# Masked attention on one core: a new order and new queues for the first loads, transposes moved inside the loop, and a merged last group

## The chip, the core and the metric

The kernel runs on one core of a Trainium2 chip. The time is the device time of the run in microseconds (us), as a median over several runs. The profile is of one execution; its span is about 2 us shorter than the run's time, since it counts from the first to the last instruction. The engines are called as in the profile: PE (matrix multiply), PEld (its weight loads, which overlap it: 272.5 and 194.8 us busy in a span of 302.5 before), DVE (vector), ACT (exponential), POOL (which issues the software-queue transfers), SP (which issues the stores).

## The reference

```python
B, S, D = 2, 3328, 128            # mask: (B, S, S) fp32, 64 ones in each row
logits = np.matmul(q, k.transpose(0, 2, 1)) * D ** -0.5
logits = np.where(mask == 0, -1e9, logits)
attn = np.exp(logits - logits.max(axis=-1, keepdims=True))
return np.matmul(attn / attn.sum(axis=-1, keepdims=True), v)
```

The mask is dense in memory: 88.6 of the 98.8 MB that the kernel reads.

## The kernel before

Each batch has 26 tiles of 128 rows. A *group* is 1, 2 or 4 query tiles (128, 256 or 512 wide) and walks over the 26 key tiles, the *chunks*, two at a time. PE adds `32768 * mask` to the logits by multiplying the mask with a scaled identity; the exponential's bias takes the 32768 off again. A column of ones beside v yields the sum for the division. Loads of q, k, v and mask are cast from fp32 to bf16 by the software queue.

```python
plans = [plan_groups([256, 256, 512, 512, 512, 512, 512, 256]),
         plan_groups([512, 512, 512, 512, 512, 512, 128, 128])]
...
def emit_transposes(b, which, half):              # 4 tiles ("a quad") per PSUM slot
    for t4 in range(h0, h1, 4):
        n = min(4, h1 - t4)
        tp = main_psum.tile([P, 4, P], bf16, name="stp", bufs=3)
        for i in range(n):
            nc.tensor.transpose(tp[:, i, :], nat[:, t4 + i, :], identb)
        nc.vector.tensor_copy(dst[:, t4 : t4 + n, :], tp[:, 0:n, :])
...
for c0 in range(0, NT, CPAIR):                    # emit_group_compute, a pair of chunks
    stp = main_psum.tile([P, CPAIR, 512], fp32, name="stp", bufs=3)
    ...   # PE, per chunk: kt x qt, then one mask matmul for each query tile
    ...   # ACT: one exponential if w == 512, else one for each chunk
    ...   # PE: pt x vones for each chunk and query tile
...
qkv_b(0, "k", 0); qkv_b(0, "k", 1); qkv_b(0, "q", 0); qkv_b(0, "q", 1)
...                                               # all transposes of batch 0
emit_mask_piece(0, 0, msks0[0], 0, 2)             # first half (13 chunks) of group 0's masks
qkv_b(0, "v", 0); qkv_b(0, "v", 1)
emit_mask_piece(0, 0, msks0[0], 1, 2)
...
for g in range(ng0): ... emit_group_compute(0, g, msks0[g])
...                                               # all transposes of batch 1
for g in range(ng1): ... emit_group_compute(1, g, msks1[g])
```

The groups' logits and the quads of transposes share three PSUM slots.

The softmax here doesn't subtract the row's maximum and nothing guards it: scores larger than these inputs give would overflow.

## Time and profile before

| | |
|---|---|
| median of 5 runs | 304.53 us (304.28 to 305.94) |
| span of the profiled run | 302.5 us |
| first exponential | 19.41 us |
| end of group 0 | 33.8 us |
| a 512-wide group of four tiles | 20.17 us |
| two 128-wide groups at the end | 13.35 us |

These are lines of the page of the kernel before: busy time of each engine as a share of the span, then the span in 40 slices of 7.56 us in tenths, then the chain of work that ended last.

```profile
PE 272.5 (90%) x3224; PEld 194.8 (64%) x3224; DVE 32.7 (11%) x139; ACT 197.8 (65%) x274; POOL 70.0 (23%) x124
...
PE   0677989999999999999998999999999999999895
...
ACT  1035986766766667666882676666766766667794
...
PEclk9999999999999999999999999999999999999998
DMA  7999999999999999999999999999999995010010
...
PE 56%; ACT 28%; DMA 6%; issue 4%; POOL 3%; DVE 1%; ACTq 0%; DVEq 0%; POOLq 0%
```

PE and the DMA engines both look full. Which one holds the time? PE's stages are read best from the divisions at the end of each group. In these lines of the timeline of DVE in the kernel before (start, duration, engine, line, operation, output and input; in brackets the idle time before it and what ended that) the first division of a group stands for the group's end.

```profile
33.78 0.17 DVE L213 RECIPROCAL recip<-ov 128x1 f32<-128x1 f32 x1 [17.09 <-PE ov L202]
...
45.95 0.17 DVE L213 RECIPROCAL recip<-ov 128x1 f32<-128x1 f32 x1 [11.15 <-PE ov L202]
...
127.19 0.17 DVE L213 RECIPROCAL recip<-ov 128x1 f32<-128x1 f32 x1 [18.43 <-PE ov L202]
...
147.64 0.17 DVE L213 RECIPROCAL recip<-ov 128x1 f32<-128x1 f32 x1 [18.71 <-PE ov L202]
...
184.88 0.17 DVE L213 RECIPROCAL recip<-ov 128x1 f32<-128x1 f32 x1 [21.19 <-PE ov L202]
...
285.71 0.17 DVE L213 RECIPROCAL recip<-ov 128x1 f32<-128x1 f32 x1 [18.43 <-PE ov L202]
...
299.06 0.17 DVE L213 RECIPROCAL recip<-ov 128x1 f32<-128x1 f32 x1 [6.15 <-PE ov L202]
```

Between two 512-wide groups there are 20.17 us, while mask half-tiles follow each other every 2.0 to 2.1 us, which is 16 to 17 us for four tiles. PE, with ACT in its loop, sets the middle, and DMA keeps ahead. The time outside that pace is in three places. (1) The head, until 33.78. (2) The boundary between the batches: groups 6 and 7 of batch 0 and group 0 of batch 1 end at 147.64, 158.77 and 184.88. (3) The tail after 285.71. The head's waits are in the timeline of PEld before:

```profile
7.59 1.30 PEld L124 LDWEIGHTS <-k_nat 128*128 128x128 bf16 x13 [7.59 <-DMA k_nat<-in_k_dram]
...
16.67 0.10 PEld L172 LDWEIGHTS <-msk 128*128 128x128 bf16 x1 [0.63 <-DMA msk<-in_mask_dram]
...
18.66 0.10 PEld L172 LDWEIGHTS <-msk 128*128 128x128 bf16 x1 [1.85 <-DMA msk<-in_mask_dram]
...
27.86 0.11 PEld L172 LDWEIGHTS <-msk 128*128 128x128 bf16 x2 [2.05 <-DMA msk<-in_mask_dram]
```

The first mask halves come behind all of k and q, and the second halves, last of ten transfers, are there only at 27.86. The timeline of ACT shows the other two places: 6.06 us without an exponential at the boundary, and a tail in which 52 exponentials follow each other without a gap, 0.264 us each.

```profile
164.41 2.12 ACT L182 ACTIVATE pt<-stp,bias_tile 128x1024 bf16<-128x1024 f32 x2 [6.06 <-PE stp L172]
...
285.00 13.73 ACT L191 ACTIVATE pt<-stp,bias_tile 128x128 bf16<-128x128 f32 x52
```

### The profile page before, as it was taken

The page shows a single profiled execution, that of the slowest core. Times are in us where ns is not written, and L with a number is a line of the kernel's source. Part 1 is how long each engine was busy: PE and PEld are TensorE (multiplying, and loading weights), DVE is VectorE, ACT ScalarE, POOL GpSimd, SP SyncE. Part 2 cuts the span into 40 slices and gives each one's busy share as a digit, 9 for nine tenths or more (in the row PEclk, how much of TensorE's full clock was granted, in tenths as well). Part 3 has the DMA queues.
Part 4 walks back from the last instruction along what each step waited for, and adds up shares of the span by engine and source line. Part 5 has one row for each costly group of instructions (what it writes and reads, how often), then busy time and mean ns, then how long its engine had stood idle before and what let it go on. Part 6 is the DMA issues. An engine that isn't in the chain of part 4 may idle for free.

```text
span 302.5 us, 7431 instructions
## 1 busy us (share of the span) xinstructions
PE 272.5 (90%) x3224; PEld 194.8 (64%) x3224; DVE 32.7 (11%) x139; ACT 197.8 (65%) x274; POOL 70.0 (23%) x124
## 2 busy tenths in 40 slices
PE   0677989999999999999998999999999999999895
PEld 0555656667676766666766666667667666676662
DVE  0510101010020020100216002002020020020200
ACT  1035986766766667666882676666766766667794
POOL 9522222222222224512222222222222200000000
PEclk9999999999999999999999999999999999999998
DMA  7999999999999999999999999999999995010010
GB/s 73 190 193 214 212 215 214 214 212 216 214 213 217 214 214 217 206 189 189 214 215 214 216 211 212 218 214 213 217 214 214 217 212 124 2 37 0 11 38 9
DMA packets 42656, 53.30 MB, mean 176 GB/s; under 512 B 22656, under 2 KB 29312, under 8 KB 42624
## 3 DMA queue, kind: packets, MB, share of 16 engines
q0 software_dynamic: 35136, 49.42, 91.2%
q1 hardware_dynamic: 7488, 3.41, 5.3%
q8 instruction: 25, 0.41, 0.5%
q14 instruction: 7, 0.06, 0.0%
HBM read 98.83 MB, written 3.41 MB: 338 GB/s over the span
## 4 chain that ended last, share of the span: by engine, by line
PE 56%; ACT 28%; DMA 6%; issue 4%; POOL 3%; DVE 1%; ACTq 0%; DVEq 0%; POOLq 0%
PE ov L202 35%; ACT pt L182 25%; PE stp L172 13%; PE stp L164 8%; DMA msk<-in_mask_dram 6%; ACT pt L191 3%; POOL k_nat L110 1%; POOL vones L99 1%; POOL q_nat L110 1%; DVE qt L125 1%; POOL msk L136 1%; DVE kt L125 0%; ACTq L182 0%; DVE o_sb L215 0%; ACTq L191 0%
## 5 line engine op out<-in xcount | busy, mean ns | idle before, releaser
L182 ACT ACTIVATE pt<-stp,bias_tile 128x1024 bf16<-128x1024 f32 x143 | 152.0, 1110 | 76.2 <-PE stp L172 76.2
L172 PE MATMUL stp<-bigident,msk 128*128 128x128 bf16 x1352 | 160.4, 220 | 3.4 <-DMA msk<-in_mask_dram 3.3
L164 PE MATMUL stp<-qt,kt 128*128 128x512 bf16 (+2 forms) x416 | 139.1, 342 | 0.3 <-ACT pt L191 0.2
L202 PE MATMUL ov<-vones,pt 128*128 128x129 bf16 x1352 | 122.5, 222 | 12.2 <-ACT pt L182 1.6
L202 PEld LDWEIGHTS <-pt 128*128 128x128 bf16 x1352 | 80.0, 98 | 67.3 <-ACT pt L182 49.8
L172 PEld LDWEIGHTS <-msk 128*128 128x128 bf16 x1352 | 106.7, 98 | 24.4 <-DMA msk<-in_mask_dram 4.8
L136 POOL DMA_DIRECT2D msk<-in_mask_dram x104 | 55.2, 532 | 161.6 <-DMA msk<-in_mask_dram 108.8
L191 ACT ACTIVATE pt<-stp,bias_tile 128x256 bf16<-128x256 f32 (+1 forms) x130 | 44.7, 481 | 23.8 <-PE stp L172 21.7
L164 PEld LDWEIGHTS <-kt 128*128 128x128 bf16 x416 | 41.1, 99 | 0.1
L213 DVE RECIPROCAL recip<-ov 128x1 f32<-128x1 f32 x52 | 7.3, 158 | 246.4 <-PE ov L202 246.4
L215 DVE TENSOR_SCALAR o_sb<-ov,recip 128x128 f32<-128x128 f32 x52 | 17.2, 348 | 1.0
L124 PE MATMUL stp<-identb,k_nat 128*128 128x128 bf16 x52 | 5.8, 264 | 8.8 <-DMA k_nat<-in_k_dram 8.4
L124 PEld LDWEIGHTS <-k_nat 128*128 128x128 bf16 x52 | 4.3, 120 | 9.2 <-DMA k_nat<-in_k_dram 8.6
L125 DVE COPY kt<-stp 128x512 bf16<-128x512 bf16 (+1 forms) x16 | 5.5, 370 | 16.7 <-PE stp L124 16.7
L124 PE MATMUL stp<-identb,q_nat 128*128 128x128 bf16 x52 | 5.4, 265 | 1.8 <-DMA q_nat<-in_q_dram 1.5
L124 PEld LDWEIGHTS <-q_nat 128*128 128x128 bf16 x52 | 4.3, 121 | 3.1 <-DMA q_nat<-in_q_dram 2.1
L125 DVE COPY qt<-stp 128x512 bf16<-128x512 bf16 (+1 forms) x16 | 5.2, 369 | 1.9 <-PE stp L124 1.9
L110 POOL DMA_DIRECT2D k_nat<-in_k_dram x4 | 4.7, 1176 | 2.8 <-DMA msk<-in_mask_dram 2.8
L110 POOL DMA_DIRECT2D q_nat<-in_q_dram x4 | 4.6, 1144 | 3.0 <-DMA msk<-in_mask_dram 3.0
L99 POOL DMA_DIRECT2D vones<-in_v_dram x4 | 4.6, 1163 | 1.7 <-DMA msk<-in_mask_dram 1.7
L191 ACT ACT_TABLE_LOAD x1 | 1.3, 1283 | 1.0 <-DVE bias_tile L82 1.0
masks.py:199 POOL TENSOR_SCALAR_AFFINE_SELECT identb<-identb 128x128 bf16<-128x128 bf16 x1 | 0.3, 282 | 0.0
(9 smaller groups left out, 1.3 us busy)
## 6 DMA issues: line engine op xcount, KB each, us to landing
msk<-in_mask_dram POOLq DMA_DIRECT2D x104, 416.0 KB, 16.7
out_dram<-o_sb SPq DMA_DIRECT2D x52, 64.0 KB, 8.1
k_nat<-in_k_dram POOLq DMA_DIRECT2D x4, 416.0 KB, 12.3
q_nat<-in_q_dram POOLq DMA_DIRECT2D x4, 416.0 KB, 13.5
vones<-in_v_dram POOLq DMA_DIRECT2D x4, 416.0 KB, 16.7
```

Source lines behind the costliest of these rows:

```text
L99: nc.gpsimd.dma_start(out=voness[b][:, h0:h1, 0:P], in_=v[b, h0 * P : h1 * P, :].rearrange("(t p) d -> p t d", p=P),)
L110: nc.gpsimd.dma_start(out=nat[:, h0:h1, :], in_=src_t[b, h0 * P : h1 * P, :].rearrange("(t p) d -> p t d", p=P),)
L124: nc.tensor.transpose(tp[:, i, :], nat[:, t4 + i, :], identb)
L125: nc.vector.tensor_copy(dst[:, t4 : t4 + n, :], tp[:, 0:n, :])
L136: nc.gpsimd.dma_start(out=msks[j][:, c0:c1, :], in_=mask[b, q0 + j * P : q0 + (j + 1) * P, c0 * P : c1 * P].rearrange("p (t c) -> p t c", ...
L164: nc.tensor.matmul(stp[:, ci, 0:w], kt[:, c, :], qt[:, t0 : t0 + nsub, :], start=True, stop=False,)
L172: nc.tensor.matmul(stp[:, ci, j * P : (j + 1) * P], msks[j][:, c, :], bigident, start=False, stop=(j == nsub - 1),)
L182: nc.scalar.activation(out=pt[:, 0:ncp, :], in_=stp[:, 0:ncp, :], func=mybir.ActivationFunctionType.Exp, bias=bias_tile, scale=softmax_scale,)
L191: nc.scalar.activation(out=pt[:, ci, 0:w], in_=stp[:, ci, 0:w], func=mybir.ActivationFunctionType.Exp, bias=bias_tile, scale=softmax_scale,)
L202: nc.tensor.matmul(ovs[j // 2][:, j % 2, 0:129], pt[:, ci, j * P : (j + 1) * P], vones[:, c, 0:129], start=(c == 0 and j % 2 == 0), stop=( ...
L213: nc.vector.reciprocal(recip, ov[:, 128:129])
L215: nc.vector.tensor_scalar_mul(o_sb, ov[:, 0:P], recip)
```

## The change

Its intent is to start the first group earlier, to keep the exponentials going at the boundary, and to shorten the tail. (a) **Head:** only 4 of 26 q tiles are loaded before group 0. They and all of k come as fp32 by the hardware queues of ACT and SP and are cast by DVE. v and masks alternate on the software queue. The second part of k is transposed inside group 0, the other q tiles inside groups 1 to 3. (b) **Boundary:** batch 1's 14 quads go between the chunk pairs of groups 6 and 7. (c) **Tail:** one 256-wide group instead of two of 128.

```diff
-            plan_groups([512, 512, 512, 512, 512, 512, 128, 128]),
+            plan_groups([512, 512, 512, 512, 512, 512, 256]),
...
         for c0 in range(0, NT, CPAIR):
+            if (b, g) == (0, 0):
+                if c0 == 8:
+                    cast_hw("k", KH, NT, k1, first_copies)
+                    while quads:
+                        emit_quad(*quads.pop(0))
+            elif quads and c0 >= quads_from:
+                emit_quad(*quads.pop(0))
...
+    KH = 12
-    qkv_b(0, "k", 0)
-    qkv_b(0, "k", 1)
-    qkv_b(0, "q", 0)
-    qkv_b(0, "q", 1)
...
+    k0 = load_hw("k", 0, KH, nc.sync)
+    q0s = load_hw("q", 0, 4, nc.scalar)
+    k1 = load_hw("k", KH, NT, nc.sync)
+    load_v(0, 6)
     emit_mask_piece(0, 0, msks0[0], 0, 2)
-    qkv_b(0, "v", 0)
-    qkv_b(0, "v", 1)
+    load_v(6, 13)
     emit_mask_piece(0, 0, msks0[0], 1, 2)
...
+    load_v(13, 26)
+    emit_mask_piece(0, 1, msks0[1], 0, 2)
+    emit_mask_piece(0, 1, msks0[1], 1, 2)
+    load_q_sw(4, 8)
...
+    load_q_sw(8, 16)
+    cast_hw("q", 0, 4, q0s)
+    cast_hw("k", 0, KH, k0)
+    for quad in quads_of("q", 0, 4) + quads_of("k", 0, KH):
+        first_copies = emit_quad(*quad)
+    early_quads = {
+        0: quads_of("k", KH, NT),
+        1: quads_of("q", 4, 8),
+        2: quads_of("q", 8, 16),
+        3: quads_of("q", 16, 26),
+    }
...
-        emit_group_compute(0, g, msks0[g])
-    emit_transposes(1, "k", 0)
...
+        emit_group_compute(
+            0, g, msks0[g],
+            quads if g >= ng0 - 2 else early_quads.get(g),
+            quads_from={ng0 - 2: 16, ng0 - 1: 4}.get(g, 18),
+        )
```

More of the change, by code (lines that the diff above doesn't have):

```diff
@@ L120, in emit_transposes, with emit_quad @@
         for t4 in range(h0, h1, 4):
-            n = min(4, h1 - t4)
-            tp = main_psum.tile([P, 4, P], bf16, name="stp", bufs=3)
-            for i in range(n):
-                nc.tensor.transpose(tp[:, i, :], nat[:, t4 + i, :], identb)
-            nc.vector.tensor_copy(dst[:, t4 : t4 + n, :], tp[:, 0:n, :])
+            emit_quad(nat, dst, t4, min(4, h1 - t4))
+    def emit_quad(nat, dst, t4, n):
+        tp = main_psum.tile([P, 4, P], bf16, name="stp", bufs=3)
+        for i in range(n):
+            nc.tensor.transpose(tp[:, i, :], nat[:, t4 + i, :], identb)
+        return nc.vector.tensor_copy(dst[:, t4 : t4 + n, :], tp[:, 0:n, :])
     def emit_ones_col(b):
@@ L146, in make_group_msks, with emit_group_compute @@
         return [mask_pool.tile([P, NT, P], bf16, name="msk") for _ in range(nsub)]
-    def emit_group_compute(b, g, msks):
+    def emit_group_compute(b, g, msks, quads=None, quads_from=4):
         kt, qt, vones = kts[b], qts[b], voness[b]
@@ L223, in qkv_b, with nat_of @@
         load_qkv_half(b, which, half)
-    emit_ones_col(0)
-    qkv_b(0, "k", 0)
-    qkv_b(0, "k", 1)
-    qkv_b(0, "q", 0)
-    qkv_b(0, "q", 1)
-    emit_transposes(0, "k", 0)
-    emit_transposes(0, "k", 1)
-    emit_transposes(0, "q", 0)
-    emit_transposes(0, "q", 1)
+    def nat_of(which):
+        if (0, which) not in nat_cache:
+            nm = {"q": "q_nat", "k": "k_nat"}[which]
+            nat_cache[(0, which)] = stage_pool.tile([P, NT, P], bf16, name=nm, bufs=1)
+        return nat_cache[(0, which)]
@@ new lines, in rows_of, with load_hw, cast_hw @@
+    def rows_of(src, b, h0, h1):
+        return src[b, h0 * P : h1 * P, :].rearrange("(t p) d -> p t d", p=P)
+    def load_hw(which, h0, h1, eng):
+        st = stage_pool.tile([P, h1 - h0, P], fp32, name=f"st_{which}{h0}", bufs=1)
+        eng.dma_start(out=st, in_=rows_of({"q": q, "k": k}[which], 0, h0, h1))
+        return st
+    def cast_hw(which, h0, h1, st, behind=None):
+        cast = nc.vector.tensor_copy(nat_of(which)[:, h0:h1, :], st)
+        if behind is not None:
+            tc.add_manual_dep(
+                cast.ins,
+                behind.ins.name,
+                mybir.DependencyInfo(
+                    mybir.DependencyClass.NoSync, mybir.DependencyReason.DATA
+                ),
+                reason="keep the late cast behind the early copies",
+            )
@@ new lines, in load_v, with load_q_sw, quads_of @@
+    def load_v(h0, h1):
+        nc.gpsimd.dma_start(out=voness[0][:, h0:h1, 0:P], in_=rows_of(v, 0, h0, h1))
+    def load_q_sw(h0, h1):
+        nc.gpsimd.dma_start(out=nat_of("q")[:, h0:h1, :], in_=rows_of(q, 0, h0, h1))
+    def quads_of(which, h0, h1):
+        dst = {"q": qts[0], "k": kts[0]}[which]
+        return [(nat_of(which), dst, t4, min(4, h1 - t4)) for t4 in range(h0, h1, 4)]
+    KH = 12
+    emit_ones_col(0)
+    k0 = load_hw("k", 0, KH, nc.sync)
+    q0s = load_hw("q", 0, 4, nc.scalar)
@@ L234 @@
+    k1 = load_hw("k", KH, NT, nc.sync)
+    load_v(0, 6)
     emit_mask_piece(0, 0, msks0[0], 0, 2)
-    qkv_b(0, "v", 0)
-    qkv_b(0, "v", 1)
+    load_v(6, 13)
     emit_mask_piece(0, 0, msks0[0], 1, 2)
-    for pc in range(2):
-        emit_mask_piece(0, 1, msks0[1], pc, 2)
+    load_v(13, 26)
+    emit_mask_piece(0, 1, msks0[1], 0, 2)
+    emit_mask_piece(0, 1, msks0[1], 1, 2)
+    load_q_sw(4, 8)
     for pc in range(2):
         emit_mask_piece(0, 2, msks0[2], pc, 2)
+    load_q_sw(8, 16)
@@ L254 @@
                 qkv_b(1, b1_qkv_parts[2 * idx + 1][0], b1_qkv_parts[2 * idx + 1][1])
-        emit_group_compute(0, g, msks0[g])
-    emit_transposes(1, "k", 0)
-    emit_transposes(1, "k", 1)
-    emit_transposes(1, "q", 0)
-    emit_transposes(1, "q", 1)
+        if g == ng0 - 2:
+            quads = [
+                (nat_cache[(1, which)], dsts[1], t4, min(4, NT - t4))
+                for which, dsts in (("k", kts), ("q", qts))
+                for t4 in range(0, NT, 4)
+            ]
+        if g == 0:
+            load_q_sw(16, 26)
+        emit_group_compute(
+            0,
+            g,
+            msks0[g],
+            quads if g >= ng0 - 2 else early_quads.get(g),
+            quads_from={ng0 - 2: 16, ng0 - 1: 4}.get(g, 18),
+        )
+    for quad in quads:
+        emit_quad(*quad)
     for pc in range(2):
```

## The prediction

> **What bounds it now.** The page gives PE 90% busy, ACT 65%, and the DMA engines at nine tenths or more of nearly every slice until 253 us. Yet in steady state DMA is ahead: a 512-wide group of four mask tiles takes 20.17 us on PE (spacing of the output divisions, e.g. 66.69 to 86.86), while mask half-tiles land every 2.0 to 2.1 us, about 16.6 us a group. So the middle is bound by PE with ACT in its loop (chain of waits: PE 56%, ACT 28%, mask DMA 6%), and the removable time lies at three places in the timeline:
>
> 1. Head. Nothing but transposes runs on PE until 16.2 us; then mask waits last until 27.86, and group 0 ends at 33.8. Ten transfers must land first (four k/q halves and two v halves at 2.34 us each, four mask halves at 2.0).
> 2. Batch boundary. From the end of group 6 of batch 0 (147.64) to the end of group 0 of batch 1 (184.88) is 37.24 us. Its 256-wide group takes about 11.1 and its 512-wide one 20.17; some 6 us are the 14 serial transpose-and-copy quads (ACT idle 6.06 us before 164.41).
> 3. Tail. Two 128-wide groups take 13.35 us, bound by ACT (52 exponentials, 13.73). A 256-wide group takes 11.1 to 12.2.
>
> **What changes.**
> - Head: only q rows of 4 of 26 tiles precede group 0, saving about 3.9 us of transfer, and k comes by hardware queues that start sooner (the first software packet moves at 3.6 us). First masks should land at 9 to 11 us, not 16.7 to 18.7. But the hardware queue shares the engines with masks. [...] The trace agrees: a 128-row output store takes 2.3 us among masks, interleaved with 127 to 131 mask packets, against 0.32 us alone. So the second k part (112 rows per engine, my arithmetic) moves slowly whenever masks flow: my estimate is landing at 18 to 30 us. Group 0 stalls for it at chunk 8 to 12. The DVE casts add an estimated 1 to 2 us. I expect group 0 to end at 28 to 33 (30), a gain of about 4.
> - Early q quads: six move from the DMA-bound head into the PE-bound groups 1 to 3. A quad is 0.22 us on PE (4 x 56 ns) and takes one of three PSUM slots; estimate 0.25 us each, loss 1.5.
> - Boundary: 14 quads move into groups 6 and 7. PE waits for ACT about 0.3 us per chunk pair in the 256-wide group, so quads mostly fit there; in the 512-wide group I estimate 0.3 each. Of 6 us some 4 are gained.
> - Tail: 1.5 us gained.
>
> **Sum:** 304.5 - 4 + 1.5 - 4 - 1.5 = 296.5 us; range 290 to 302. Faster by over 2%: 0.64; within: 0.31; slower: 0.05.
>
> **What would show it.** First exponential before 13 us (was 19.4); first output division near 30 (33.8). A PE wait on the k copies or casts inside group 0. Group 6 to batch 1 group 0 about 33 us, with no 6 us ACT idle; groups 2 and 3 about 0.5 to 0.8 longer than 20.17; last group about 12 us. DMA bytes written up by about 1 MB, ending near 250.
>
> **What would make it wrong.** Masks starving the second k part past 30 us: group 0 then ends no earlier, and the head gains nothing. Quads stalling the PSUM rotation by more than 0.5 us each: the boundary gain goes. In the other direction: hardware rows that keep pace with the masks (group 0 ending at 27) and quads that fit wholly into PE's waits would give 290.

## The result, and the profile after

The changed kernel takes 296.67 us (median of 8 runs, 296.51 to 296.87); the kernel before, in the same rounds, 304.53 (15 runs). The ratio is 0.9729, 95% interval 0.9713 to 0.9746. All ratios here are the mean time of one kernel's fast runs over that of the other's of the same rounds, so not quite the ratio of the medians.

The same lines of the page of the changed kernel:

```profile
PE 266.5 (90%) x3198; PEld 192.0 (65%) x3198; DVE 36.0 (12%) x138; ACT 195.8 (66%) x248; POOL 69.6 (24%) x124
...
PE   0499999999999999999999999999999999999994
...
ACT  1068876667676767666777767676766667676784
...
PEclk9999999999999999999999999999999999999997
DMA  7999999999999999999999999999999999410010
...
PE 52%; ACT 29%; DMA 11%; issue 4%; POOL 2%; ACTq 1%; DVE 0%; POOLq 0%
```

The shares of busy time hardly moved, and the idle slices at the start became fewer. In the chain that ended last DMA has 11% instead of 6%. The list of that chain in order of time (start, duration) shows why. Before, one mask load stands in it, from 10.22 us for 17.59 us. After, there are two, one after the other:

```profile
6.82 17.96 DMA msk<-in_mask_dram
25.07 15.79 DMA msk<-in_mask_dram
```

The second ends in a PE wait at 40.90, for a mask of group 2. So in this profile the chain runs through the arrival of masks up to there, and not through the work of groups 0 and 1. The stages tell more. The divisions in the timeline of DVE after:

```profile
28.96 0.17 DVE L222 RECIPROCAL recip<-ov 128x1 f32<-128x1 f32 x1 [8.29 <-PE ov L211]
...
41.62 0.17 DVE L222 RECIPROCAL recip<-ov 128x1 f32<-128x1 f32 x1 [4.42 <-PE ov L211]
...
123.62 0.17 DVE L222 RECIPROCAL recip<-ov 128x1 f32<-128x1 f32 x1 [18.43 <-PE ov L211]
...
144.74 0.17 DVE L222 RECIPROCAL recip<-ov 128x1 f32<-128x1 f32 x1 [2.73 <-PE ov L211]
...
179.16 0.17 DVE L222 RECIPROCAL recip<-ov 128x1 f32<-128x1 f32 x1 [19.74 <-PE ov L211]
...
280.17 0.17 DVE L222 RECIPROCAL recip<-ov 128x1 f32<-128x1 f32 x1 [18.44 <-PE ov L211]
...
291.27 0.17 DVE L222 RECIPROCAL recip<-ov 128x1 f32<-128x1 f32 x1 [9.38 <-PE ov L211]
```

Differences of such lines give the table, in us from one group's end to the next; "batch 1, group 0" includes what was left of the boundary.

| stage | before | after | change |
|---|---|---|---|
| until the end of group 0 | 33.78 | 28.96 | -4.82 |
| group 1 (256 wide, 1 quad moved in) | 12.17 | 12.66 | +0.49 |
| group 2 (2 quads) | 20.74 | 21.12 | +0.38 |
| group 3 (3 quads) | 20.17 | 20.54 | +0.37 |
| group 6 (5 quads) | 20.45 | 21.12 | +0.67 |
| group 7 (256 wide, 9 quads) | 11.13 | 13.67 | +2.54 |
| batch 1, group 0 | 26.11 | 20.75 | -5.36 |
| tail (two groups, then one), to its last group's division | 13.35 | 11.10 | -2.25 |

The seven other groups moved by at most 0.15 us. Head -4.8, moved q quads +1.2, boundary -2.2, tail -2.2, and +0.3 in the rest and the last stores: that is the 7.7 us between the spans. Not all of the 1.2 us is the quads' price: 0.46 of group 1's 0.49 is the wait at 40.90, the last line below. In `e3_head`, a run below with the same quads and without that wait, the three groups grew by 0.11, 0.37 and 0.36 us, 0.8 together. The head's waits, in the timeline of PEld after:

```profile
7.18 0.34 PEld L126 LDWEIGHTS <-q_nat 128*128 128x128 bf16 x4 [7.18 <-DVE q_nat L249]
8.05 1.20 PEld L126 LDWEIGHTS <-k_nat 128*128 128x128 bf16 x12 [0.52 <-DVE k_nat L249]
...
13.06 0.24 PEld L181 LDWEIGHTS <-msk 128*128 128x128 bf16 x3 [3.35 <-DMA msk<-in_mask_dram]
14.93 0.10 PEld L181 LDWEIGHTS <-msk 128*128 128x128 bf16 x1 [1.64 <-DMA msk<-in_mask_dram]
...
40.90 0.10 PEld L181 LDWEIGHTS <-msk 128*128 128x128 bf16 x1 [0.46 <-DMA msk<-in_mask_dram]
```

PE waits for q and the first k until 8.05, then for the first masks until 13.06 and 14.93. The second k part doesn't appear as a wait at all: DVE began to cast it at 15.49, as soon as it had landed and before group 0 could use it. One more thing slows the head, which the page does not show (its PEclk row reads 9 from the start): PE itself. In the same timeline a weight load takes 0.15 us at first and 0.10 us later:

```profile
16.84 0.15 PEld L173 LDWEIGHTS <-kt 128*128 128x128 bf16 x1
...
20.12 0.10 PEld L173 LDWEIGHTS <-kt 128*128 128x128 bf16 x1
```

The change comes at 18.8 us, and at 23.2 in the kernel before. It comes at 17.9, 18.0 and 20.5 us in three other profiles with the same head (`e6_octets`, `e7_twice`, `e3_head`, all below), where group 0 ended at 28.60, 28.66 and 29.67. Weight loads are slower again in `e1_tail` (below) where the granted clock dips: 30 of them keep PEld busy for 2.75 us there, at a granted 0.68, and 48 for 2.77 in `e2_boundary`, at 1.00. So this looks like PE's clock. Group 0's end thus carries a spread of about 1 us that no edit made. The tail in the timeline of ACT after has one short gap and 26 exponentials:

```profile
279.45 3.02 ACT L200 ACTIVATE pt<-stp,bias_tile 128x256 bf16<-128x256 f32 x8
282.98 7.92 ACT L200 ACTIVATE pt<-stp,bias_tile 128x256 bf16<-128x256 f32 x18 [0.50 <-PE stp L181]
```

### The profile page after: what moved, and what is told of

The parts are those of the page before. It is cut to its first block, busy times and chain, and to the rows that moved or that the text cites. A ratio compares the mean times of both kernels' runs of the same rounds, so it can differ in the third digit from the quotient of the medians.

```text
span 294.8 us, 7345 instructions
## 1 busy us (share of the span) xinstructions
PE 266.5 (90%) x3198; PEld 192.0 (65%) x3198; DVE 36.0 (12%) x138; ACT 195.8 (66%) x248; POOL 69.6 (24%) x124
## 4 chain that ended last, share of the span: by engine, by line
PE 52%; ACT 29%; DMA 11%; issue 4%; POOL 2%; ACTq 1%; DVE 0%; POOLq 0%
PE ov L211 32%; ACT pt L191 26%; PE stp L181 12%; DMA msk<-in_mask_dram 11%; PE stp L173 7%; ACT pt L200 3%; POOL vones L261 1%; POOL msk L138 1%; PE stp L126 1%; ACTq L191 0%; DVE o_sb L224 0%; ACTq L366 0%; DVE recip L222 0%; POOL identb masks.py:199 0%; POOL bigident L71 0%
## 5 line engine op out<-in xcount | busy, mean ns | idle before, releaser
L181 PE MATMUL stp<-bigident,msk 128*128 128x128 bf16 x1352 | 158.0, 220 | 4.3 <-DMA msk<-in_mask_dram 4.3
L173 PE MATMUL stp<-qt,kt 128*128 128x512 bf16 (+1 forms) x390 | 136.6, 353 | 0.1
L211 PE MATMUL ov<-vones,pt 128*128 128x129 bf16 x1352 | 118.1, 222 | 12.7 <-ACT pt L191 1.6
L211 PEld LDWEIGHTS <-pt 128*128 128x128 bf16 x1352 | 78.4, 98 | 64.6 <-ACT pt L191 47.0
L138 POOL DMA_DIRECT2D msk<-in_mask_dram x104 | 56.1, 540 | 158.0 <-DMA msk<-in_mask_dram 110.6
L200 ACT ACTIVATE pt<-stp,bias_tile 128x256 bf16<-128x256 f32 x104 | 42.1, 476 | 21.6 <-PE stp L181 18.7
L173 PEld LDWEIGHTS <-kt 128*128 128x128 bf16 x390 | 38.4, 99 | 0.1
L264 POOL DMA_DIRECT2D q_nat<-in_q_dram x3 | 2.6, 868 | 4.1 <-DMA msk<-in_mask_dram 3.1
L110 POOL DMA_DIRECT2D k_nat<-in_k_dram x2 | 2.3, 1145 | 4.8 <-issue 2.8
L249 DVE CAST k_nat<-st_k 128x1536 bf16<-128x1536 f32 (+1 forms) x2 | 2.0, 1024 | 5.5 <-DMA st_k<-in_k_dram 5.5
```

What stands on the lines that cost most here:

```text
L138: nc.gpsimd.dma_start(out=msks[j][:, c0:c1, :], in_=mask[b, q0 + j * P : q0 + (j + 1) * P, c0 * P : c1 * P].rearrange("p (t c) -> p t c", ...
L173: nc.tensor.matmul(stp[:, ci, 0:w], kt[:, c, :], qt[:, t0 : t0 + nsub, :], start=True, stop=False,)
L181: nc.tensor.matmul(stp[:, ci, j * P : (j + 1) * P], msks[j][:, c, :], bigident, start=False, stop=(j == nsub - 1),)
L200: nc.scalar.activation(out=pt[:, ci, 0:w], in_=stp[:, ci, 0:w], func=mybir.ActivationFunctionType.Exp, bias=bias_tile, scale=softmax_scale,)
L211: nc.tensor.matmul(ovs[j // 2][:, j % 2, 0:129], pt[:, ci, j * P : (j + 1) * P], vones[:, c, 0:129], start=(c == 0 and j % 2 == 0), stop=( ...
L264: nc.gpsimd.dma_start(out=nat_of("q")[:, h0:h1, :], in_=rows_of(q, 0, h0, h1))
```

## The experiments

All twelve gave correct results and ran beside the kernel before on the same chip.

### One part at a time

`e1_tail`, `e2_boundary` and `e3_head` are the kernel before with one of the three parts:

```diff
 e1_tail:     plan_groups([512, 512, 512, 512, 512, 512, 256])     # nothing else
 e2_boundary: before's head and tail; quads of batch 1 in groups 6 and 7
 e3_head:     before's tail and boundary; new loads, casts, q quads in groups 1 to 3
```

> Only the last plan changes: one 256-wide group for two of 128. If the three parts of the change are independent, the time falls by the 2.2 us that the tail gained in the two profiles (285.71 to 302.5 before, 280.17 to 294.8 after): ratio about 0.993. If the tail's gain was only the shorter wait after other parts moved, less than 1 us.

> Only the transposes of batch 1 move into groups 6 and 7 of batch 0. By the profiles the boundary gained 57.69 - 55.54 = 2.15 us from group 6 to the first group of batch 1: ratio about 0.993. The prediction's 4 us would give 0.987.

> Only the head changes (order of loads, hardware queues and casts, late q transposes). By the profiles group 0 ends 4.8 us earlier and groups 1 to 3 lose 1.2 us: net 3.6 us, ratio about 0.988. The three parts should sum to the whole, 7.9 us, within 0.6 us.

| run | median us (range) | ratio to before (95%) |
|---|---|---|
| `e1_tail` | 303.09 (302.43 to 304.21) | 0.994 (0.9901 to 0.998) |
| `e2_boundary` | 303.0 (302.23 to 303.94) | 0.9944 (0.9901 to 0.9987) |
| `e3_head` | 300.26 (300.2 to 300.51) | 0.9845 (0.9815 to 0.9875) |

The savings add: 0.6 + 0.56 + 1.55 = 2.71%, the same as the whole. The stages agree: in `e1_tail` the tail's group takes 11.10 us; in `e2_boundary` the three boundary stages take 21.39 + 13.66 + 20.74; in `e3_head` group 0 ends at 29.67. The 0.987 that the prediction's 4 us at the boundary would give lies outside `e2_boundary`'s interval. The head is more than half of it. The first two intervals are wide, about 1.2 us to each side, so the sum alone does not prove that the parts are independent.

Those wide intervals show something else. With the old head, runs fall on two levels, in the kernel before too: of the 7 runs beside these, four lie at 304.16 to 304.42 and three at 305.5 to 306.0. The profile of `e1_tail` caught an upper run (304.21), that of `e2_boundary` a lower one (302.23). These are windows of 4 us around the end of the last mask wait (the stretch and its length; busy us and number of instructions of PE, PEld, DVE, ACT and POOL; granted clock of PE; DMA share; GB/s), first `e1_tail`:

```profile
24.00:28.00 4.00, 1.88 (x22) 1.03 (x19) 0.00 (x0) 1.23 (x4) 0.79 (x2) 1.00 1.07 212
28.00:32.00 4.00, 3.42 (x29) 2.75 (x30) 0.00 (x0) 3.06 (x8) 1.06 (x2) 0.68 1.08 213
32.00:36.00 4.00, 4.00 (x51) 3.39 (x50) 0.44 (x3) 3.33 (x10) 1.06 (x2) 0.89 1.07 212
```

and then `e2_boundary`:

```profile
24.00:28.00 4.00, 2.76 (x32) 2.08 (x30) 0.00 (x0) 1.68 (x4) 0.63 (x2) 1.00 1.07 211
28.00:32.00 4.00, 3.85 (x50) 2.77 (x48) 0.00 (x0) 3.85 (x11) 1.06 (x2) 1.00 1.07 211
32.00:36.00 4.00, 3.90 (x51) 2.88 (x51) 0.94 (x4) 3.74 (x11) 1.06 (x2) 1.00 1.07 212
```

In the upper run PE was granted 0.68 and 0.89 of its clock in the 8 us after the wait, and group 0 ended at 35.52 instead of 33.74. Of these 1.78 us some 0.6 are the mask's own lateness (the wait ended at 28.45 against 27.82). The record agrees for the other runs: the mean granted clock of every upper run is 0.989 to 0.994, that of every lower one 0.995 to 0.999. The same dip stands in two more profiles, `e9_late_one_exp` (0.89 and 0.68 from 24 to 32 us) and `e11_quarters_two_exp` (0.61 from 24 to 28; its weight loads take 0.15 us from 23.88 to 27.00). The runs of `e3_head` and of the changed kernel lie within 0.4 us of each other; they have no such wait amid group 0. That is worth more than the stages of the profile (a lower-level run) show: part of `e3_head`'s 1.55% is these slow starts. Within a level, `e1_tail` and `e2_boundary` are each 1.8 to 2.0 us below the kernel before (302.43 and 302.23 against 304.3), and `e3_head` is 4.0 below it. Together that is 7.8 us, where the changed kernel is 7.7 below: within a level the parts do add. Why one run falls on the upper level and another on the lower was not tested.

### Hardware queues or order?

`e4_head_sw` keeps the new order, but uses the software queue alone:

```diff
-    k0 = load_hw("k", 0, KH, nc.sync)
-    q0s = load_hw("q", 0, 4, nc.scalar)
-    k1 = load_hw("k", KH, NT, nc.sync)
+    load_sw("q", 0, 4)          # cast by the DMA, into q_nat and k_nat
+    load_sw("k", 0, KH)
+    load_sw("k", KH, NT)
...                              # the three DVE casts go
```

> The changed kernel, but all first k and q loads go in the same order by the software queue, cast by the DMA, with no DVE casts. Theory A (the head gained by the hardware queues starting early, at 1.7 us instead of 3.6): group 0 ends about 2 us later than in the changed kernel, near 31, ratio to before about 0.98. Theory B (it gained by putting fewer bytes before the masks, whichever queue carries them): group 0 ends within 0.7 us of 28.96, ratio about 0.973.

It took 297.93 us (297.75 to 298.09), ratio 0.9767; group 0 ended at 29.84. Of the head's 4.8 us, 3.9 are still there (33.78 - 29.84), and the hardware queues are worth at most about 1 us: 0.9 in group 0's end, 1.3 in the medians (with intervals that overlap). That is nearer theory B, but a little outside its 0.7. Against the four profiles with the hardware queues, where group 0 ended at 28.60 to 29.67 and group 1 at 41.62 to 41.95, it is 0.2 to 1.2 us (29.84) and 0.3 to 0.6 us (42.23), so the exact size is not settled. The order of bytes is most of the gain. In the trace, the hardware queues move their first row at 1.8 us and the software queue here at 3.2; yet PE has the first k part at 8.05 with them and at 8.34 without.

### What stands before the masks

The prediction feared that masks would starve the second k part. The profile after shows the reverse. `e5_k1_late` puts that part behind the first masks:

```diff
-    k1 = load_hw("k", KH, NT, nc.sync)
-    load_v(0, 6)
     emit_mask_piece(0, 0, msks0[0], 0, 2)
+    load_v(0, 6)
+    load_sw("k", KH, NT)
```

> The changed kernel, but the second part of k goes by the software queue, cast by the DMA, behind the first mask halves and the first part of v; the rest of the order stays. Theory A (group 0 starts when its first masks land, and the second k part stands ahead of them, 112 rows per engine or about 2.5 to 3 us): the first exponential comes near 12.5 to 13.5 us instead of 15.7, group 0 ends near 26.5 instead of 28.96, the time is near 294.5. Rival (all bytes that group 0 needs must land anyway, and it ends when the last of them has): the first exponential is earlier, but group 0 waits for k or the later masks inside and ends within 0.6 us of 28.96, time within 0.6 us of 296.7.

It took 295.76 us (295.68 to 295.99), ratio 0.9693. The waits of PEld, in its timeline:

```profile
10.35 0.10 PEld L180 LDWEIGHTS <-msk 128*128 128x128 bf16 x1 [0.29 <-DMA msk<-in_mask_dram]
...
13.99 0.17 PEld L126 LDWEIGHTS <-k_nat 128*128 128x128 bf16 x3 [0.40 <-DMA k_nat<-in_k_dram]
...
19.29 0.10 PEld L180 LDWEIGHTS <-msk 128*128 128x128 bf16 x1 [1.72 <-DMA msk<-in_mask_dram]
...
39.92 0.10 PEld L180 LDWEIGHTS <-msk 128*128 128x128 bf16 x1 [1.14 <-DMA msk<-in_mask_dram]
```

PE's last wait for the first mask halves ends at 10.35 instead of 14.93, and the first exponential comes at 11.11 instead of 15.69, earlier than theory A expected. Theory A's cause is right, but its size is not: group 0 ends at 27.28, a gain of 1.7, not 2.5, because it now waits for k (0.40) and for the second mask half (1.72). Group 1 takes 13.35 instead of 12.66 because a mask of group 2 is late (1.14). Of 4.6 us at the start, 0.9 are left in the time. The rest fits the rival: past the start, PE waited inside the groups for bytes that landed later (the 0.40, 1.72 and 1.14 us above).

### What a quad costs at the boundary

The boundary gained 2.2 us and not 4. Its three stages still cost 4.1 us more than 20.17 + 11.1 + 20.17. Two causes were possible: PE's own time, or the PSUM slot that each quad takes from the rotation. `e6_octets` keeps the 52 transposes but uses 8 slots instead of 14; `e7_twice` keeps the slots and doubles the transposes.

```diff
 e6_octets:
-        tp = main_psum.tile([P, 4, P], bf16, name="stp", bufs=3)
+        tp = main_psum.tile([P, max(n, 4), P], bf16, name="stp", bufs=3)
...
-                (nat_cache[(1, which)], dsts[1], t4, min(4, NT - t4))
+                (nat_cache[(1, which)], dsts[1], t8, min(8, NT - t8))
 e7_twice:
         for i in range(n):
-            nc.tensor.transpose(tp[:, i, :], nat[:, t4 + i, :], identb)
+            for _ in range(2 if dst is kts[1] or dst is qts[1] else 1):
+                nc.tensor.transpose(tp[:, i, :], nat[:, t4 + i, :], identb)
```

> The changed kernel, but the transposes of batch 1 go eight to a PSUM slot with one copy, so 8 slots instead of 14, with the same 52 transposes. Groups 6, 7 and the first of batch 1 take 21.12 + 13.67 + 20.75 = 55.54 us in the changed kernel, some 4.1 more than 20.17 + 11.1 + 20.17. If that cost is PSUM slots taken out of the rotation, it falls with their number, to about 2.3 (sum 53.8, time near 295). If it is PE time (52 x 56 ns = 2.9 us), the sum stays within 0.5 us of 55.5.

> The changed kernel, but each transpose of batch 1 is done twice into the same place: 52 more transposes (2.9 us of PE at 56 ns), same slots and copies. If the boundary's remaining cost is PE time, the sum of the three groups rises by about 2.9 us to 58.4 and the time to 299.5. If PE has waits into which they fit and slots are the cost, it rises by less than 1 us.

| run | group 6 | group 7 | batch 1, group 0 | sum | median us |
|---|---|---|---|---|---|
| changed kernel | 21.12 | 13.67 | 20.75 | 55.54 | 296.67 |
| `e6_octets` | 22.15 | 12.76 | 20.75 | 55.66 | 297.03 (ratio 0.9733) |
| `e7_twice` | 22.83 | 15.14 | 20.75 | 58.72 | 299.91 (ratio 0.9828) |

Fewer slots changed nothing. 52 more transposes cost 3.18 us, 61 ns each, a little more than the 56 ns at which transposes follow each other on PE in the trace. So it is PE's time, and over the three stages it counts in full: about 2.9 of the 4.1 us left. It is not spread evenly: the 20 further transposes in group 6 cost 1.71 us (86 ns each), the 32 in group 7 cost 1.47 (46 ns each), so in group 7 a small part does hide. What makes up the other 1.2 us was not tested. The lines of `e7_twice` behind the sum, with the timeline of DVE as above:

```profile
123.71 0.17 DVE L223 RECIPROCAL recip<-ov 128x1 f32<-128x1 f32 x1 [18.43 <-PE ov L212]
...
146.54 0.17 DVE L223 RECIPROCAL recip<-ov 128x1 f32<-128x1 f32 x1 [3.03 <-PE ov L212]
...
161.68 0.17 DVE L223 RECIPROCAL recip<-ov 128x1 f32<-128x1 f32 x1 [3.73 <-PE ov L212]
...
182.43 0.17 DVE L223 RECIPROCAL recip<-ov 128x1 f32<-128x1 f32 x1 [19.73 <-PE ov L212]
```

### A version that beats both: shorter loops, then finer loads

`e8_one_exp` changes the 256-wide groups, which no part of the change touched: one exponential for a pair of chunks.

```diff
-            if w == 512:
-                ...                 # one exponential
-            else:
-                for ci in range(ncp):
-                    ...             # one for each chunk
+            nc.scalar.activation(out=pt[:, 0:ncp, 0:w], in_=stp[:, 0:ncp, 0:w], ...)
```

> The changed kernel, but the 256-wide groups do one exponential per pair of chunks (128x512 elements) instead of two. From starts of back-to-back exponentials (0.264 us at 128 columns, 0.384 at 256, 1.06 at 1024) I estimate 0.61 us instead of 0.77 a pair. If ACT's time bounds these groups, each of the four shortens by up to 2 us (13 pairs x 0.16): time near 289 to 292, last group near 9.5 instead of 11.10. If the loop PE-ACT-PE bounds them, the later start of the exponential (it waits for both chunks) cancels it: within 1 us of 296.7, or slower.

295.26 us (293.81 to 295.36), ratio 0.9664. Group 7 took 12.23 instead of 13.67 and the last 10.03 instead of 11.10: 1.44 and 1.07 us. An exponential of 128x512 takes 0.68 us, and back to back it starts 0.585 us after the one before it, so the 0.61 that I estimated was close. But in the second half of the last group the exponentials start 0.77 to 0.80 us apart, against 0.97 for a pair of two in the changed kernel: 0.18 a pair, and 1.07 us over the whole group. What holds them at 0.79 was not tested. Group 1 ended no earlier (41.55 against 41.62): PE waited 1.87 us for a mask of group 2 there. Here, too, runs fall on two levels, 293.81 once and 295.2 to 295.36 three times; the head has waits again.

`e9_late_one_exp` joins the last two. `e10_quarters` also brings the masks of groups 0 to 2 in quarters; `e11_quarters_two_exp` is that with the two exponentials of before; `e12_early_qk` moves three loads of q and k ahead of masks.

```diff
 e10_quarters, against e9_late_one_exp:
-    emit_mask_piece(0, 0, msks0[0], 0, 2)
+    emit_mask_piece(0, 0, msks0[0], 0, 4)
     load_v(0, 6)
+    emit_mask_piece(0, 0, msks0[0], 1, 4)
     load_sw("k", KH, NT)
     load_v(6, 13)
-    emit_mask_piece(0, 0, msks0[0], 1, 2)
+    emit_mask_piece(0, 0, msks0[0], 2, 4)
     load_v(13, 26)
+    emit_mask_piece(0, 0, msks0[0], 3, 4)
...                                     # groups 1 and 2 in quarters as well
 e12_early_qk, against e10_quarters:
+        if pc == 3:                    # before group 1's last quarter
+            load_q_sw(4, 8)
...
+        if pc == 2:                    # before group 2's last half
+            load_q_sw(8, 16)
...
-        if pf < ng0: ...               # masks of group 7, then k of batch 1
+        if pf >= ng0 - 1: ...          # k of batch 1 first
```

> The later second k part and the single exponential together, on the changed kernel. If groups 0 and 1 are now held by the arrival of masks (group 1 ended at 40.6 to 41.6 in all variants, with a mask wait of 1.1 to 1.9 us just after it), the two gains don't add in the head: group 1 ends near 40.5, and only groups 7 and the last keep their 2.5 us: time near 293 (295.76 - 2.5). If they add, group 1 ends near 39 and the time is under 292.

> As the run before, but the masks of groups 0, 1 and 2 come in quarters of 6 or 7 chunks instead of halves of 13, in the same order otherwise. If arrival of whole halves holds the first groups, PE starts and continues earlier with the same bytes: first exponential near 9.5 to 10.5 us (11.1), group 1 ends by 39, time near 291 to 292. If the rate of bytes itself holds them, the end of group 2 stays within 0.5 us of the run before.

> Quarters and later second k part, but two exponentials per pair in the 256-wide groups, as in the changed kernel. Separates the quarters from the single exponential: time near 294 to 294.5 if the quarters gain 1 to 1.5 us on 295.76; group 7 and the last group stay at 13.7 and 11.1.

> The run with quarters, but the loads that its transposes waited for go earlier: q tiles 8 to 15 before the last half of group 2's masks, q tiles 4 to 7 before the last quarter of group 1's, k of batch 1 before group 7's masks. If those waits (1.2 us on q in group 2, 1.5 us on k in group 6) are what made group 2 take 23.32 and group 6 22.21 us, they return to about 21.1 each, and the time falls from 293.1 to about 290. If the bytes moved ahead only delay masks that PE then waits for, it stays within 0.7 us of 293.1.

| run | median us (range) | ratio to before (95%) | end of group 0 | of group 1 | of group 2 | group 6 |
|---|---|---|---|---|---|---|
| changed kernel | 296.67 (296.51 to 296.87) | 0.9729 (0.9713 to 0.9746) | 28.96 | 41.62 | 62.74 | 21.12 |
| `e9_late_one_exp` | 293.35 (292.91 to 294.46) | 0.9627 (0.9592 to 0.9662) | 27.68 | 40.65 | 61.77 | 21.12 |
| `e10_quarters` | 293.09 (292.7 to 293.35) | 0.9609 (0.9585 to 0.9632) | 25.75 | 36.85 | 60.17 | 22.21 |
| `e11_quarters_two_exp` | 295.67 (295.43 to 295.74) | 0.9693 (0.967 to 0.9715) | 27.66 | 38.68 | 60.05 | 22.48 |
| `e12_early_qk` | 291.65 (291.57 to 292.07) | 0.9562 (0.9532 to 0.9591) | 26.24 | 37.23 | 60.52 | 21.12 |

`e9_late_one_exp` behaved as a head held by arriving masks should: group 1 ended at 40.65, and the gains didn't add there. `e10_quarters` brought group 1's end forward by 3.8 us, yet the time by only 0.3. Two lines of its list of waits (who waited for whom; us in total, times, longest) show where the rest went:

```profile
PEld L126 <- DMA k_nat<-in_k_dram: 2.8, 2, 1.5
...
PEld L126 <- DMA q_nat<-in_q_dram: 1.9, 2, 1.2
```

The longest of each is 1.2 us in group 2, before q tiles that came late (at 50.54), and 1.5 us in group 6, before batch 1's k (at 132.27). PE, now early, waited for loads whose place in the queue had been good enough before. `e11_quarters_two_exp` missed its expectation: it came out no faster than `e5_k1_late` (295.76), because group 2 ended 1.7 us earlier (60.05 against 61.75), but group 6 took 22.48 against 21.12. (Its end of group 0 is not to be set against that of `e10_quarters`: its profile has the dip of the clock from 24 to 28 us.) `e12_early_qk` hit half of its own: group 6 went back to 21.12, which is 1.1 of the 1.4 us gained, but group 2 stayed at 23.29, with a wait for a mask of 0.76 us at 47.37 in place of the wait for q, and a longer one, 1.65 us at 59.19 (1.30 at 58.85 in `e10_quarters`), for a mask of group 3. In these runs PE waited for bytes early in the program, whichever load was put last. `e12_early_qk` is the fastest kernel: 5.0 us below the changed kernel by the medians (of different calls) and 4.4% below the kernel before by the ratio.

## Why the prediction was right or wrong

**The sum was right, partly by errors that cancel.** It said 296.5 us; 296.67 were measured. By parts: head -4 (measured -4.8), q quads +1.5 (+1.2, of which about 0.4 is a mask wait), boundary -4 (-2.2), tail -1.5 (-2.2 by the stages, about -1.9 by `e1_tail` within a level).

**"Only q rows of 4 of 26 tiles precede group 0, saving about 3.9 us": right.** `e4_head_sw` has this and no hardware queue, and group 0 ended 3.9 us earlier. (v was split and moved among the masks at the same time, so the two are not separated.)

**"The second k part moves slowly whenever masks flow ... landing at 18 to 30 us. Group 0 stalls for it": wrong.** It had landed by 15.49, and group 0 stalled for masks. The alternation was read rightly from the stores (124 to 131 mask packets to most stores of 128 rows), but here it began late. In the changed kernel the software queue moved its first row at 7.0 us (3.6 before). By then two thirds of k's 3328 rows were through (2211 packets by 7.0 us). What was left did move slowly among the masks, as predicted: 132 packets of it from 10.5 us to its last at 15.1. But that was early enough for group 0. So k delayed the masks, which came at 13.06 and 14.93 and not at "9 to 11"; `e5_k1_late` shows it by taking k away from there.

**"The DVE casts add an estimated 1 to 2 us": the size was right (0.98 and 0.94 us for the first two), the cost was not.** PE waited for masks after them, so they were hidden.

**"PE waits for ACT about 0.3 us per chunk pair in the 256-wide group, so quads mostly fit there": this is the step that failed.** Nine quads lengthened group 7 by 2.54 us, 0.28 each, and `e7_twice` charged the further transposes to the time, in full over the boundary and at 46 of 56 ns in this group. The wait was not spare time. In this group PE's weight loads waited 2.2 us in all for exponentials before, 3.1 with the quads and 3.2 with twice the transposes (the lists of waits of these windows), so the wait did not shrink when work was put in. This fits a loop in which PE works in order: what is put before the next logits delays the next exponential too, and with it the next wait. The boundary gains the serial part (copies and restart), not PE's time for the transposes. Group 6, with 0.13 us a quad, was cheaper (0.19 against the 20.17 of the other groups) than the 0.3 that I assigned to it.

**The tail was undersized:** I took 11.1 to 12.2 us for the last group; it was 11.10. That ACT bounded the two 128-wide groups agrees with its gapless 13.73 us.

**Not foreseen:** some of the old kernel's runs (three of the seven above, at a mean granted clock of 0.992 against 0.996 to 0.998) are slow, as `e1_tail` was after its mask wait, and the changed kernel's runs show no second level. Nor did I foresee that masks would still hold PE at 40.90, so that time gained in groups 0 and 1 is partly lost there.

## What to carry to other kernels

When a head is bound by transfers, ask what stands in the queues before the first byte that the first group needs. Order the loads by need, whichever queue carries them, and look in the trace whether the queue that filled first held the other up, as it seems to have done here (first software row at 7.0 us instead of 3.6). A wait inside a PE-ACT loop may not be a free slot, as here: price work that moves there at its full PE time (61 ns a transpose here, against 56 from one to the next in the trace), and test that by doubling it. When one stage has become faster, look at once for the loads that were only just early enough for the slow one.

## What the traces show of the queues and the clock

- Among masks the rows of two queues alternated: a store of 128 rows took about 2.3 us with 124 to 131 mask packets between them in most stores of the kernel before, and 0.33 to 0.35 us without masks. But the queue that started second didn't get its turn at once in the changed kernel. The software queue's first row moved at 3.6 us before, at 3.2 in `e4_head_sw` and at 7.0 in the changed kernel, where it was issued at 1.63 us as in the kernel before (1.62) behind a hardware queue that had moved its first row at 1.84. Between 7.0 and 7.5 us it got 69 packets against 214, and from 8.0 to 8.5 an even 138 against 137. In `e5_k1_late`, with less in the hardware queue, it moved its first row at 5.4 us. That the full queue is the cause was not tested alone.
- From the start of the issue to the first packet in the trace there were 2.0 us on the software queue (1.62 to 3.60, before) and 1.1 us on the hardware queue (0.74 to 1.84, after). The issue is a good part of that: before, it lasted from 1.62 to 2.89, and the first packet moved 0.7 us after its end.
- In `e1_tail` the granted clock was 0.68 in the 4 us after a PE wait of 2.50 us, with 1.88 us of PE work from 24 to 28 us. In the kernel before, a wait of 1.82 us at the same place left it at 1.00. The runs of the kernel before fell on two levels some 1.4 us apart (304.16 to 304.42 and 305.5 to 306.0). What length of wait, or what else, brings the lower clock was not tested.
